# A hybrid decoder layer on one core: products of q's and k's norms three block products behind, a second buffer for u3 in the second set, k's normalisation written beside the last 16 pairs

## The chip, the cores and the metric

The kernel runs on one core of one Trainium2 chip. The metric is the device time of one execution in microseconds (us). Before the change it is 2805.34 us, the median of three runs (2804.27 to 2805.68). One further execution was profiled; it took 2804.28 us. Everything below is float32, computed as products of a rounded high part and a low part (`hi`, `lo`), so that each product of matrices is three matmuls.

## The reference, cut to what matters

```python
h = rms_norm(x, ln_gain)                       # x: 1024 x 2048
proj = h @ w_in                                # 2048 x 10240
q, k, v, z_att, u, z_ssm, g_att, g_ssm = split(proj)   # 1024 wide each, g_*: 2048
q = rms_norm(q.reshape(.., 8, 2, 64), q_norm_gain)
k = rms_norm(k.reshape(.., 8, 2, 64), k_norm_gain)
attn = rms_norm(diff_attention(q, k, v, lam), subln_gain) * (1 - lam_init)
y_att = attn * silu(z_att)
y_ssm = s5_branch(u, ...) * silu(z_ssm)
m = sigmoid(g_att) * (y_att @ w_pa) + sigmoid(g_ssm) * (y_ssm @ w_ps)
x = x + m @ w_out
```

The change touches the first product, `h @ w_in`, in the half of it that finishes the columns, and the root mean squares of q and k that are taken while those columns come out.

## The kernel before

**Tiling.** `h @ w_in` is made in pairs of column blocks: 40 pairs n of 256 columns, and for each pair two halves of the 2048 rows of `w_in`. A pair of one half is a two-by-two block product done in Strassen's manner, with seven block products instead of eight (`pair`, L502). A block product is a call of `products` (L486): 12 matmuls of 128x512 into one PSUM bank. The seven of a pair run in this written order: A11 into bank `pa`, S2 into `pb`, then the last two (A22 and S4) of the pair before, then A12 into `pa`, S1 into `pc`, S3 into `pb`. After A11, S2 and S3 ScalarE copies the bank to SBUF, as `p1`, `u2` and `u3`; the trace names these tiles `p` and `u`. A22 of a pair adds to the same bank `pb` out of which `u3` was just copied, so it can't start before that copy (L523) is done.

**Two sets.** In the first set the pairs are multiplied with one half of the rows and their four outputs go to DRAM (`part`, d_p). In the second set, 36 pairs that are called in the loop at L1044, the same pairs are multiplied with the other half; the first half's output comes back into a tile `q` (L555), is added on GpSimd and VectorE, and each of the four outputs of a pair is handed to a function of its kind (`whole`, L548). In order of the loop's index i: q (4 pairs), k (4), v (4), z_att (4), z_ssm (4), g_att (8), g_ssm (8).

**What is done with the outputs.** For q, `evac_q` (L986) scales and splits the output into `sh_` (ScalarE, L990) and `sl_` (VectorE, L991), stores both, and calls `norms` (L968). For k, `evac_k` stores the output and calls `norms`. `norms` squares the output (`sq`), splits the square into another `sh_` and `sl_` (L90, L91), and adds two matmuls (L975) with a selecting matrix that sum the squares into a bank `nps`. There are two buffers of `sh_` and one of `sl_`. v is transposed and split; z_att and z_ssm go through a sigmoid and a multiplication on GpSimd (L1034, L1035); the gates g through a sigmoid.

**The normalisation of k.** `qk_norms` (L953) makes the inverse root mean squares from `nps`. `norms_k` (L999) is a generator of 16 steps: load a block of k and its factors (`ks`, `rb`; one buffer each), multiply on VectorE (L1015), split into `sh_` and `sl_`, store both, load the next.

**What sets the order.** In this stage each engine's instruction stream is laid out when the program is built, by a scheduler which goes by the dependencies and a timeline of its own; an instruction that stands late in the text is placed early where its inputs are there early. On the chip each engine runs its stream in that order. All DMAs are issued on SyncE's queue, in order too.

Of the kernel before, what the change touches and what calls it, by code (L numbers as in the profile page):

```python
# [10 lines left out]
F32 = mybir.dt.float32  # L11
F32R = mybir.dt.float32r
# [7 lines left out]
P = 128  # L20
# [47 lines left out]
def hybrid_block(ctx: ExitStack, tc: tile.TileContext, x_t, x_n, w_t, w_v, w_glu, w_pa, w_ps,  # L68
                 w_out, small, lams, ssm_bc, out):
    nc = tc.nc  # L70
    V, A, Q, T, D = nc.vector, nc.scalar, nc.gpsimd, nc.tensor, nc.sync
# [17 lines left out]
    def split(hi, lo, src, eng=None):  # L89
        A.activation(hi, src, AF.Copy)  # L90
        (eng or V).tensor_tensor(lo, src, hi.bitcast(F32), ALU.subtract)  # L91
# [11 lines left out]
    def newton_rsqrt(pool, y, v, n):  # L103

        s = pool.tile(list(v.shape), F32, name=n + "_s", tag=n + "_s", bufs=1)
        yi = y.bitcast(I32)
        V.tensor_scalar(yi, v.bitcast(I32), 1, None, ALU.arith_shift_right)
        V.tensor_scalar(yi, yi, -1.0, float(0x5F3759DF), ALU.mult, ALU.add)
        for _ in range(4):
            V.tensor_tensor(s, y, y, ALU.mult)  # L110
            V.tensor_tensor(s, s, v, ALU.mult)
            V.tensor_scalar(s, s, -0.5, 1.5, ALU.mult, ALU.add)
            V.tensor_tensor(y, y, s, ALU.mult)
# [90 lines left out]
    sel = const.tile([P, 160], F32R, name="sel")  # L204
# [55 lines left out]
    def run(steps):  # L260
        for _ in steps:
            pass
# [63 lines left out]
    with ExitStack() as pa_ctx:  # L326
        wp = pa_ctx.enter_context(tc.tile_pool(name="wp", bufs=1, side="right"))
        post = pa_ctx.enter_context(tc.tile_pool(name="post", bufs=1, side="right"))
# [154 lines left out]
        def gain(k):  # L483
            return sm[:, C_LNG + k:C_LNG + k + 1]

        def products(ps, i, a, w, start):  # L486
            hs, ls = a
            wh, wl = w[i]
            for j in range(4):
                c = slice(j * P, (j + 1) * P)  # L490
                for n, (x, y) in enumerate(((wh, hs), (wh, ls), (wl, hs))):
                    T.matmul(ps, lhsT=x[:, c], rhs=y[i][j], start=(start and j == 0 and n == 0),  # L492
                             stop=(j == 3 and n == 2), skip_group_check=True)

        pending = []

        def finish():

            if pending:
                pending.pop()()  # L500

        def pair(w, a, out11, out21, out22, out12):  # L502


            def bank():
                return acc.tile([P, 512], F32, name="acc", tag="acc")
            pa = bank()
            products(pa, A11, a, w, True)
            p1 = post.tile([P, 512], F32, name="p1", tag="p1", bufs=2)
            A.activation(p1, pa, AF.Copy)  # L510
            pb = bank()
            products(pb, S2, a, w, True)
            u2 = post.tile([P, 512], F32, name="u2", tag="u2", bufs=2)
            A.activation(u2, pb, AF.Copy)  # L514
            finish()
            products(pa, A12, a, w, False)
            out11(pa)
            pc = bank()
            products(pc, S1, a, w, True)
            V.tensor_tensor(pc, pc, p1, ALU.subtract)  # L520
            products(pb, S3, a, w, False)
            u3 = post.tile([P, 512], F32, name="u3", tag="u3")
            A.activation(u3, pb, AF.Copy)  # L523
            out22(pc, u3)

            def rest():
                products(pb, A22, a, w, False)
                out21(pb, p1)
                products(pc, S4, a, w, False)
                out12(pc, u2)  # L530
            pending.append(rest)
# [410 lines left out]
        xp_ctx.close()  # L942
        ev_ctx = ExitStack()
        stg = ev_ctx.enter_context(tc.tile_pool(name="stg", bufs=2, side="right"))
        qp = ev_ctx.enter_context(tc.tile_pool(name="qp", bufs=8, side="right"))


        rq = const.tile([P, 16, NT], F32, name="rq")
# [1 line left out]
        nps = [sps.tile([P, 512], F32, name=f"nps{t}", tag=("v", "y")[t]) for t in range(2)]  # L950
        n_norms = [0, 0]

        def qk_norms():  # L953

            for t in range(2):
                v = stg.tile([32, 512], F32, name="nv", tag="sq")
                y = stg.tile([32, 512], F32, name="ny", tag="ny", bufs=1)
                V.tensor_scalar(v, nps[t][0:32], 1.0 / 64, EPS, ALU.mult, ALU.add)
                newton_rsqrt(stg, y, v, "nr")
                D.dma_start(d_rk[:, t * 512:(t + 1) * 512], y[16:32])  # L960
                yield
                tp = sps.tile([P, 4, 32], F32, name="rqp", tag="tr", bufs=2)
                for j in range(4):
                    T.transpose(tp[:, j], y[:, j * P:(j + 1) * P], ident[0:32, 0:32])
                V.tensor_copy(rq[:, :, 4 * t:4 * t + 4].rearrange("p a t -> p t a"), tp[:, :, 0:16])
            V.tensor_scalar(nrq, rq, -1.0, None, ALU.mult)

        def norms(src, row, t):  # L968

            sq = stg.tile([P, 512], F32, name="sq", tag="sq")  # L970
            A.activation(sq, src, AF.Square)
            hi, lo = split_tiles()
            split(hi, lo, sq)
            for n, m in enumerate((hi, lo)):
                T.matmul(nps[t], lhsT=sel[:, 32 - row:160 - row], rhs=m,  # L975
                         start=(n_norms[t] == 0), stop=(n_norms[t] == 31), skip_group_check=True)
                n_norms[t] += 1

        def store2(dst, hi, lo):
            for d_, s_ in zip(dst, (hi, lo)):  # L980
# [2 lines left out]
        def split_tiles():  # L983
            return (stg.tile([P, 512], F32R, name="sh_", tag="sh_"),
                    stg.tile([P, 512], F32R, name="sl_", tag="sl_", bufs=1))
# [9 lines left out]
        def evac_k(h, t, st):  # L995
            D.dma_start(d_k[h, :, t * 512:(t + 1) * 512], st)
            norms(st, 16 + 2 * h, t)
# [46 lines left out]
        for i, (kind, n) in enumerate(order):  # L1044
            f, m = evacs[kind], n - first[kind]
            whole(n, a, 0, lambda c, t, st, f=f, m=m: f(2 * m + c, t, st), qp, None, w)
            w = None
            if n == 8:
                steps = qk_norms()
            if n in (8, 10, 12):  # L1050
                next(steps, None)
            if i == 12:
                ks = norms_k()
            if i >= 12:
                next(ks, None)
        finish()
        ev_ctx.close()
        hp_ctx.close()
        sps_ctx.close()
# [52 lines left out]
        for t in range(2):  # L1112
            tk = slice(t * 512, (t + 1) * 512)
            ya = act_half(act, yg_inputs(t))
            for ct in range(8):
# [3 lines left out]
                for b in range(2):  # L1119
                    raw = wp.tile([P, 4, P], F32, name="w_raw", tag="w_raw", bufs=5)  # L1120
                    D.dma_start(raw, w_glu[ct, :, 4 * b:4 * b + 4])
                    m = (2 * ct + b) % 7
                    hi, lo = (wp.tile([P, 4, P], F32R, name=n, tag=f"{n}{m}") for n in ("w_hi", "w_lo"))
# [15 lines left out]
                hi, lo = (gl.tile([P, 512], F32R, name=n, tag=n, bufs=2) for n in ("yh", "yl"))  # L1139
# [13 lines left out]
    with ExitStack() as at:  # L1153
# [111 lines left out]
        with tc.manual_schedule(engines={T.engine}):  # L1265
            for h in range(H):
# [3 lines left out]
                for n, tt in enumerate(ORDER):  # L1270
                    i = h * NT + n
# [62 lines left out]
    for t in range(2):  # L1334
# [14 lines left out]
        for cb in range(4):  # L1349
            ps = [po.tile([P, 512], F32, name="o", tag="o") for _ in range(4)]  # L1350
            for k in range(KT):
                wh, wl = load_w(w_out[cb, :, k:k + 1], 1, None, wp2)
                for i in range(4):
                    tt = slice(i * P, (i + 1) * P)
                    for n, (a, w) in enumerate(((mh, wh), (mh, wl), (ml, wh))):
                        T.matmul(ps[i], lhsT=a[k][:, tt], rhs=w[:, 0],  # L1356
                                 start=(k == 0 and n == 0), stop=(k == KT - 1 and n == 2))
# [82 lines left out]
```

## Time and profile before

| what | value |
|---|---|
| median of 3 runs | 2805.34 us |
| the profiled execution | 2804.28 us |
| its span, first to last instruction | 2802.5 us |
| TensorE's mean granted clock | 0.985 |
| matmul records in the span | 12402 |
| first and last row of k's multiplication (L1015) | 1253.0 and 1423.9 us |

The span is the time between the first and the last instruction of the profiled execution, 1.8 us less than its own time. In the second set the outputs of q come out in the stretch from some 1000 to 1120 us, those of z_att and z_ssm between some 1290 and 1430 us, and the last 16 pairs after that. Busy time of TensorE in the profile is a union of overlapping matmuls, so a stretch that is 100% busy may still hold matmuls at half the granted clock; the count of matmuls in a stretch tells more than its busy share.

### The profile page before, as it was taken

How to read it: one execution, taken by the hardware profiler on the slowest of the kernel's cores; microseconds unless marked ns; L12 is line 12 of the kernel's file. 1: busy time of each engine (PE TensorE's matmuls, PEld its weight loads, DVE VectorE, ACT ScalarE, POOL GpSimd, SP SyncE). 2: the span in 40 equal slices, each digit the busy share in tenths (PEclk: the TensorE clock that was granted, in tenths of full speed). 3: DMA queues.
4: the chain of work that ended last, by engine and by line, in shares of the span. 5: the costliest groups of instructions: out<-in, count | busy, mean ns of one | idle time of the engine just before them, and what ended most of it. 6: DMA issues, size and time to landing. Idle time of an engine off the chain costs nothing. (4 is left out here: it accounts for less than half of the span.)

```text
span 2802.5 us, 37947 instructions
## 1 busy us (share of the span) xinstructions
PE 2695.5 (96%) x12402; PEld 2205.5 (79%) x12402; DVE 1844.1 (66%) x3512; ACT 1205.9 (43%) x2359; POOL 743.7 (27%) x1101
## 2 busy tenths in 40 slices
PE   9999999999999998998899999789999999999999
PEld 8888788887878876776678888667878778888887
DVE  4998877777787776787676666457666575325432
ACT  6433455545455544433444444345555433223221
POOL 0002866565674011224442222212222200000000
PEclk9999999999999999999999999999999999999999
DMA  9653333333333454457765555976777386455453
GB/s 350 220 180 115 103 113 117 115 116 120 121 101 117 166 181 165 149 174 230 243 214 167 168 162 169 317 234 194 198 238 206 128 296 194 131 155 177 150 158 113
DMA packets 261926, 487.82 MB, mean 174 GB/s; under 512 B 33912, under 2 KB 44480, under 8 KB 261728
## 3 DMA queue, kind: packets, MB, share of 16 engines
q1 hardware_dynamic: 261728, 485.40, 53.7%
q8 instruction: 98, 1.61, 0.2%
q14 instruction: 100, 0.82, 0.1%
HBM read 345.72 MB, written 139.56 MB: 173 GB/s over the span
## 5 line engine op out<-in xcount | busy, mean ns | idle before, releaser
L492 PE MATMUL acc<-ah,w_hi 128*128 128x512 f32 x2128 | 841.6, 396 | 28.1 <-ACT u L523 22.8
L492 PE MATMUL acc<-ah,w_lo 128*128 128x512 f32 x2128 | 841.0, 396 | 0.0
L492 PE MATMUL acc<-al,w_hi 128*128 128x512 f32 x2128 | 840.2, 395 | 0.0
L90 ACT ACTIVATE w_hi<-w_raw 128x512 fp32r<-128x512 f32 x532 | 333.9, 629 | 523.3 <-PE o L1356 219.7
L91 DVE TENSOR_TENSOR w_lo<-w_raw,w_hi 128x512 fp32r<-128x512 f32 x474 | 338.4, 715 | 308.9 <-ACT w_hi L90 296.3
L492 PEld LDWEIGHTS acc<-ah,w_hi 128*128 128x128 f32 x2128 | 402.7, 189 | 120.6 <-ACT u L523 27.6
L492 PEld LDWEIGHTS acc<-ah,w_lo 128*128 128x128 f32 x2128 | 402.5, 189 | 87.7 <-issue 5.4
L492 PEld LDWEIGHTS acc<-al,w_hi 128*128 128x128 f32 x2128 | 402.9, 189 | 83.4 <-issue 2.0
L90 ACT ACTIVATE w_hi<-value 128x512 fp32r<-128x512 f32 x304 | 191.7, 630 | 313.3 <-DVE value L346 161.4
L91 DVE TENSOR_TENSOR w_lo<-value,w_hi 128x512 fp32r<-128x512 f32 x304 | 219.5, 722 | 61.3 <-ACT w_hi L90 53.7
L1356 PE MATMUL o<-w_lo,mh 128*128 128x512 f32 x512 | 199.2, 389 | 0.0
L1356 PE MATMUL o<-w_hi,ml 128*128 128x512 f32 x512 | 199.2, 389 | 0.0
L1356 PE MATMUL o<-w_hi,mh 128*128 128x512 f32 x512 | 195.3, 389 | 0.0
L581 POOL TENSOR_TENSOR u<-u,q 128x512 f32<-128x512 f32 x72 | 99.8, 1387 | 230.2 <-ACT u L514 120.7
L346 DVE TENSOR_TENSOR value<-w_raw 128x512 f32<-128x512 f32 x152 | 150.3, 989 | 2.7
L1185 DVE TENSOR_SCALAR_CACHE_REDUCE pe<-s,nrq 128x128 f32<-128x128 f32 (+7 forms) x128 | 100.1, 813 | 70.9 <-PE s L1181 58.9
L91 POOL TENSOR_TENSOR w_lo<-w_raw,w_hi 128x512 fp32r<-128x512 f32 x58 | 84.0, 1448 | 234.3 <-ACT w_hi L90 204.0
L575 POOL TENSOR_TENSOR p<-p,q 128x512 f32<-128x512 f32 x36 | 60.5, 1680 | 322.5 <-DVE acc L520 210.0
L288 PE MATMUL pc<-ah,w_hi 128*128 128x512 f32 x256 | 107.6, 420 | 25.4 <-DVE z L292 16.8
L1187 ACT ACTIVATE pe<-pe,mx 128x128 f32<-128x128 f32 (+7 forms) x128 | 98.5, 773 | 42.2 <-DVE pe L1185 42.0
L1356 PEld LDWEIGHTS o<-w_lo,mh 128*128 128x128 f32 x512 | 96.1, 188 | 20.0
L1356 PEld LDWEIGHTS o<-w_hi,mh 128*128 128x128 f32 x512 | 96.1, 188 | 19.9
(681 smaller groups left out, 4588.5 us busy)
## 6 DMA issues: line engine op xcount, KB each, us to landing
w_raw<-in_w_t_dram SPq DMA_DIRECT2D x288, 256.0 KB
q<-d_p SPq DMA_DIRECT2D x160, 256.0 KB
w_raw<-in_w_out_dram SPq DMA_DIRECT2D x128, 256.0 KB
d_p<-u SPq DMA_DIRECT2D x72, 256.0 KB
w_raw<-in_w_ps_dram SPq DMA_DIRECT2D x64, 256.0 KB
w_raw<-in_w_pa_dram SPq DMA_DIRECT2D x64, 256.0 KB
d_p<-ps SPq DMA_DIRECT2D x52, 256.0 KB
d_p<-p SPq DMA_DIRECT2D x36, 256.0 KB
```

Source lines behind the costliest of these rows:

```text
L90: A.activation(hi, src, AF.Copy)
L91: (eng or V).tensor_tensor(lo, src, hi.bitcast(F32), ALU.subtract)
L288: T.matmul(ps, lhsT=w[:, k % 4], rhs=b[k], start=(k == 0 and n == 0), stop=(k == 7 and n == 2))
L346: V.tensor_tensor(t, x, y, ALU.add)
L492: T.matmul(ps, lhsT=x[:, c], rhs=y[i][j], start=(start and j == 0 and n == 0), stop=(j == 3 and n == 2), skip_group_check=True)
L575: e.tensor_tensor(u, u, other(1), ALU.add)
L581: e.tensor_tensor(u, u, other(i), ALU.subtract)
L1185: V.tensor_scalar(pc[c][:, 0:w], sc[c][:, 0:w], nrq[:, 2 * h + c, tt:tt + 1], None, ALU.mult, ALU.min, accum_out=mx[:, c:c + 1])
L1187: ins = A.activation(pc[c][:, 0:w], pc[c][:, 0:w], AF.Exp, bias=mx[:, c:c + 1], scale=-1.0, accum_out=su[:, c:c + 1])
L1356: T.matmul(ps[i], lhsT=a[k][:, tt], rhs=w[:, 0], start=(k == 0 and n == 0), stop=(k == KT - 1 and n == 2))
```

## The change

There are four edits.

1. `norms` no longer places its two matmuls at once. It appends them to a list, and `products` emits what is due: a matmul pair is emitted at the start of the third block product after the one that is current. The square's parts get tiles of their own, `nh` and `nl`, two buffers each, so that `sh_` and `sl_` are left to `evac_q`, `evac_v` and `norms_k`.
2. In the second set `u3` is taken in turns from the old place and from a second one, so there are two buffers.
3. To make room, the tiles `q` get 5 buffers in place of 8, and `ny` shares a buffer with `rb`.
4. `qk_norms` starts one pair later (its inputs come later), and `norms_k` is started at i = 20 in place of i = 12; its last step is run after the loop.

```diff
+        tick, postponed = [0], []
+
         def products(ps, i, a, w, start):
+            tick[0] += 1
+            while postponed and postponed[0][0] <= tick[0]:
+                postponed.pop(0)[1]()
...
-        pending = []
+        pending, turn, more = [], [0], []
...
-            u3 = post.tile([P, 512], F32, name="u3", tag="u3")
+            turn[0] ^= 1
+            if more and turn[0]:
+                u3 = more[0].tile([P, 512], F32, name="u3", tag="u3", bufs=1)
+            else:
+                u3 = post.tile([P, 512], F32, name="u3", tag="u3")
...
-        qp = ev_ctx.enter_context(tc.tile_pool(name="qp", bufs=8, side="right"))
+        more.append(stg)
+        qp = ev_ctx.enter_context(tc.tile_pool(name="qp", bufs=5, side="right"))
...
-                y = stg.tile([32, 512], F32, name="ny", tag="ny", bufs=1)
+                y = stg.tile([32, 512], F32, name="ny", tag="rb", bufs=1)
...
-            hi, lo = split_tiles()
+            hi, lo = (stg.tile([P, 512], F32R, name=n, tag=n) for n in ("nh", "nl"))
             split(hi, lo, sq)
-            for n, m in enumerate((hi, lo)):
-                T.matmul(nps[t], lhsT=sel[:, 32 - row:160 - row], rhs=m,
-                         start=(n_norms[t] == 0), stop=(n_norms[t] == 31), skip_group_check=True)
-                n_norms[t] += 1
+
+            def add():
+                for m in (hi, lo):
+                    T.matmul(nps[t], lhsT=sel[:, 32 - row:160 - row], rhs=m,
+                             start=(n_norms[t] == 0), stop=(n_norms[t] == 31), skip_group_check=True)
+                    n_norms[t] += 1
+            postponed.append((tick[0] + 3, add))
...
-            if n == 8:
+            if n == 9:
                 steps = qk_norms()
-            if n in (8, 10, 12):
+            if n in (9, 11, 13):
                 next(steps, None)
-            if i == 12:
+            if i == 20:
                 ks = norms_k()
-            if i >= 12:
+            if i >= 20:
                 next(ks, None)
         finish()
+        run(ks)
```

The changed program's lines are numbered higher: L497 is the matmul of `products`, L987 that of the norms, L1004 evac_q's low part, L1028 k's multiplication.

**First place: TensorE, in the q pairs.** Before, in the third q pair: the end of S3 into bank acc_11394, four matmuls of the norms, and A22 into the same bank.

```order
L492 MATMUL acc_11394<-al_10952,w_hi_11366 128x512
L492 MATMUL acc_11394<-ah_10951,w_lo_11367 128x512
L975 MATMUL nps0_11009<-sl__11252,sel_65 128x512
L975 MATMUL nps0_11009<-sh__11278,sel_65 128x512
L975 MATMUL nps0_11009<-sl__11279,sel_65 128x512
L975 MATMUL nps1_11010<-sh__11322,sel_65 128x512
L492 MATMUL acc_11394<-ah_10960,w_hi_11371 128x512
L492 MATMUL acc_11394<-al_10961,w_hi_11371 128x512
```

After, one pair further on: the end of S3 into acc_11600, with the start of A11 of the next pair into acc_11791.

```order
L987 MATMUL nps0_11009<-nh_11665,sel_65 128x512
L497 MATMUL acc_11600<-al_10952,w_hi_11570 128x512
L497 MATMUL acc_11600<-ah_10951,w_lo_11571 128x512
L497 MATMUL acc_11791<-ah_10845,w_hi_11756 128x512
L497 MATMUL acc_11791<-al_10846,w_hi_11756 128x512
L497 MATMUL acc_11791<-ah_10845,w_lo_11757 128x512
L497 MATMUL acc_11791<-ah_10849,w_hi_11756 128x512
L497 MATMUL acc_11791<-al_10850,w_hi_11756 128x512
L987 MATMUL nps0_11009<-nl_11666,sel_65 128x512
L497 MATMUL acc_11791<-ah_10849,w_lo_11757 128x512
```

Before, S3 and A22 of a pair stand back to back with only the norms' matmuls between them. After, A11 and S2 of the next pair, 24 matmuls, stand between S3 and A22, and the norms' matmuls are strewn among the products: those of S4's output, `nh_11665` and `nl_11666`, have 36 and 44 matmuls between them and the end of that S4.

**Second place: VectorE, in the q pairs.** Before, the low parts of q (L991) and of its square (L91) take the one `sl_` buffer in turn.

```order
L991 SCALAR_TENSOR_TENSOR sl__11452<-u2_11199,gqk_66,sh__11451 128x512
L91 TENSOR_TENSOR w_lo_11959<-w_raw_11952,w_hi_11958 128x512
L91 TENSOR_TENSOR sl__11460<-sq_11457,sh__11459 128x512
L991 SCALAR_TENSOR_TENSOR sl__11479<-q_11328,gqk_66,sh__11478 128x512
L91 TENSOR_TENSOR w_lo_11783<-value_11780,w_hi_11782 128x512
L346 TENSOR_TENSOR value_11962<-w_raw_11950,w_raw_11952 128x512
L91 TENSOR_TENSOR sl__11487<-sq_11484,sh__11486 128x512
```

After, `sl_` is q's alone, and the square's low part is `nl`.

```order
L1004 SCALAR_TENSOR_TENSOR sl__11658<-u2_11405,gqk_66,sh__11657 128x512
L580 TENSOR_TENSOR q_11532<-acc_11583,q_11532 128x512
L91 TENSOR_TENSOR w_lo_11769<-w_raw_11754,w_hi_11768 128x512
L91 TENSOR_TENSOR nl_11666<-sq_11663,nh_11665 128x512
L1004 SCALAR_TENSOR_TENSOR sl__11683<-q_11532,gqk_66,sh__11682 128x512
L525 TENSOR_TENSOR acc_11694<-acc_11694,p1_11598 128x512
L91 TENSOR_TENSOR w_lo_11773<-value_11760,w_hi_11772 128x512
```

The number of instructions is the same; between two uses of the `sl_` buffer there are now three other instructions, and none of them takes the buffer.

**Third place: VectorE, where k is multiplied.** Before, in the third pair of z_att (i = 14):

```order
L1015 TENSOR_TENSOR ks_14247<-ks_14247,rb_14249 128x512
L366 TENSOR_TENSOR value_13914<-value_13914,w_raw_13906 128x512
L571 TENSOR_TENSOR q_13712<-acc_13763,q_13712 128x512
L91 TENSOR_TENSOR w_lo_13921<-w_raw_13906,w_hi_13920 128x512
L91 TENSOR_TENSOR sl__14422<-ks_14247,sh__14421 128x512
L520 TENSOR_TENSOR acc_13846<-acc_13846,p1_13776 128x512
L91 TENSOR_TENSOR w_lo_13925<-value_13912,w_hi_13924 128x512
L346 TENSOR_TENSOR value_13928<-w_raw_13900,w_raw_13904 128x512
L91 TENSOR_TENSOR w_lo_13931<-value_13928,w_hi_13930 128x512
L1015 TENSOR_TENSOR ks_14427<-ks_14427,rb_14429 128x512
```

After, in the fourth pair of z_att (i = 15):

```order
L1028 TENSOR_TENSOR ks_15555<-ks_15555,rb_15557 128x512
L366 TENSOR_TENSOR value_14053<-value_14053,w_raw_14045 128x512
L580 TENSOR_TENSOR q_13863<-acc_13914,q_13863 128x512
L91 TENSOR_TENSOR w_lo_14060<-w_raw_14045,w_hi_14059 128x512
L91 TENSOR_TENSOR sl__15722<-ks_15555,sh__15721 128x512
L525 TENSOR_TENSOR acc_13997<-acc_13997,p1_13927 128x512
L91 TENSOR_TENSOR w_lo_14064<-value_14051,w_hi_14063 128x512
L346 TENSOR_TENSOR value_14067<-w_raw_14039,w_raw_14043 128x512
L91 TENSOR_TENSOR w_lo_14070<-value_14067,w_hi_14069 128x512
L1028 TENSOR_TENSOR ks_15727<-ks_15727,rb_15729 128x512
```

Nothing moved within the piece; it stands one pair later. Counted by the rows of pc - p1 (L520, L525), of which every pair has one, 76 in all and 36 in the second set, the 16 multiplications of k stand before behind the 52nd to the 59th such row, and after behind the 54th to the 60th. Those are the pairs i = 12 to 19 before (from the second step on i = 13) and i = 14 to 20 after, z_att and z_ssm but for the last, though the changed text starts `norms_k` at i = 20. The order of ScalarE and SyncE there is likewise the same but for the shift, and behind the second set all streams stand as before, but for an exchange of neighbours here and there. Between its first and its last multiplication of k VectorE's stream has now 123 rows for 16 steps; before, it had 118 from the second step to the sixteenth.

## The prediction

> **What bounds the kernel now.** I read the page first, then the busy time by stretches, then what TensorE (PE) waits for in the stretches that lose time, and last the timelines behind those waits. The page gives the frame:
>
> ```profile
> PE 2695.5 (96%) x12402; PEld 2205.5 (79%) x12402; DVE 1844.1 (66%) x3512; ACT 1205.9 (43%) x2359; POOL 743.7 (27%) x1101
> ```
>
> TensorE is the bound; only the time in which it stands or runs slowly can be won. Four stretches of the second set, with each engine's busy time and count, the granted clock and the share of DMA:
>
> ```profile
> 975.00:1130.00 155.00, 137.53 (x558) 108.94 (x557) 109.84 (x152) 74.28 (x129) 26.11 (x18) 0.93 0.50 168
> 1130.00:1200.00 70.00, 70.00 (x313) 57.59 (x312) 49.63 (x69) 34.22 (x60) 14.75 (x10) 1.00 0.42 140
> 1290.00:1430.00 140.00, 119.32 (x484) 93.46 (x483) 97.68 (x126) 54.42 (x97) 58.11 (x42) 0.95 0.74 240
> 1430.00:1700.00 270.00, 270.00 (x1192) 223.54 (x1192) 180.65 (x231) 120.19 (x201) 68.27 (x48) 1.00 0.53 169
> ```
>
> The last is undisturbed: 270 us / 1192 matmuls = 0.2265 us for one, and 84 x 0.2265 = 19.03 us for a pair. At that pace the 558 matmuls of the first stretch (q) would take 126.4 us of 155, so 28.6 us are lost there; the 484 of the third (z_att and z_ssm) 109.6 of 140, so 30.4. Together 59.0 us, 2.1% of the span, are the most that the edits can touch. What PE waits for, in the first stretch and then in z_att and z_ssm:
>
> ```profile
> PE acc L492 <- ACT u L523: 5.9, 5, 1.5
> PE nps L975 <- DVE sl__11279 L91: 3.5, 1, 3.5
> PE nps L975 <- DVE sl__11695 L91: 3.5, 1, 3.5
> PE nps L975 <- DVE sl__11487 L91: 3.4, 1, 3.4
> ```
> ```profile
> PE acc L492 <- ACT u L523: 15.8, 6, 4.3
> PE acc L492 <- DVE q L571: 3.1, 4, 1.6
> ```
>
> The waits in the first make some 16 us, not 28.6. PE's timeline shows the rest:
>
> ```profile
> 1035.74 0.40 PE L975 MATMUL nps<-sh__11278,sel 128*128 128x512 f32 x1
> 1039.68 0.50 PE L975 MATMUL nps<-sl__11279,sel 128*128 128x512 f32 x1 [3.54 <-DVE sl__11279 L91]
> 1042.33 0.80 PE L492 MATMUL acc<-ah,w_hi 128*128 128x512 f32 x1 [1.41 <-ACT u L523]
> 1043.34 0.63 PE L492 MATMUL acc<-ah,w_lo 128*128 128x512 f32 x1
> 1043.77 0.63 PE L492 MATMUL acc<-ah,w_hi 128*128 128x512 f32 x1
> 1048.31 0.40 PE L492 MATMUL acc<-ah,w_hi 128*128 128x512 f32 x1
> ```
>
> After the wait a matmul starts every 0.43 us (1043.34 to 1043.77) instead of 0.23, until 1048.31: a long wait is followed by some 5 us at half the clock, which costs 2 to 3 us more.
>
> **Term 1: q's norms (edits 1 and 2).** Why was `sl__11487`, the low part of a square, late?
>
> ```profile
> 1065.60 0.75 DVE L991 SCALAR_TENSOR_TENSOR sl__11479<-q,gqk,sh__11478 128x512 fp32r<-128x512 f32 x1 [2.25 <-PE nps L975]
> 1068.49 0.69 DVE L91 TENSOR_TENSOR sl__11487<-sq,sh__11486 128x512 fp32r<-128x512 f32 x1 [0.81 <-DMA d_q<-sl__11479]
> ```
> ```profile
> 1066.37 0.32 SPq L981 DMA_DIRECT2D d_q<-sl__11479  x1
> ```
>
> The one buffer goes from VectorE to a store, back to VectorE, to PE and back: VectorE waits for PE's norm matmul, then for the store (issued at 1066.37, done when the next row starts, 2.1 us later), and PE waits for VectorE. The order puts exactly these matmuls between S3 and A22, where PE has nothing else. The change takes both away. The squares get `nh` and `nl`, held only until PE has read them. The norms' matmuls have 36 and 44 others between them and the product whose square they sum: 36 x 0.2265 = 8.2 us. The chain they wait for is an output's VectorE operation, the square, its copy and its low part, four operations of 0.6 to 0.75 us, so some 3 us; 5 us remain for what queues ahead on ACT and DVE. And S3 and A22 of a pair have 24 matmuls between them, 5.4 us, for the copy of u3 to come. No arithmetic is added: the same 64 norm matmuls stay on PE's path. The most won is 28.6 us. The least: DVE works 109.8 of 155 us there and keeps `sl_` in one buffer for q, so each of the four q pairs could still lose a wait as long as those of 3.5 us with some 2.5 us of half clock, 4 x 6 = 24 us; only 4 to 5 us would be won. I take 4 us left (a wait of 1 us in each q pair, without the half clock), nearer to the upper end, because the k pairs, whose squares take the same path without a store of `sl_`, lose nothing (313 matmuls in the 70 us of the second row above): **-24.6 us**.
>
> **Term 2: k's normalisation (edit 4).** The stretch of z_att and z_ssm loses its time otherwise. One of its stalls, on DVE, ACT and PE:
>
> ```profile
> 1319.59 0.69 DVE L1015 TENSOR_TENSOR ks<-ks,rb 128x512 f32<-128x512 f32 x1 [3.26 <-DMA ks<-d_k]
> 1324.42 1.64 DVE L346 TENSOR_TENSOR value<-w_raw 128x512 f32<-128x512 f32 x1
> ```
> ```profile
> 1326.15 0.63 ACT L90 ACTIVATE w_hi<-value 128x512 fp32r<-128x512 f32 x1 [3.42 <-DVE value L346]
> 1326.69 0.58 ACT L523 ACTIVATE u<-acc 128x512 f32<-128x512 f32 x1
> ```
> ```profile
> 1327.32 0.50 PE L492 MATMUL acc<-ah,w_hi 128*128 128x512 f32 x1 [2.72 <-ACT u L523]
> ```
>
> PE names u3's copy, but ACT was held in its order by a weight's copy, that by a sum on DVE, and DVE by `ks`, whose load was late. k's multiplications run as a loop: load, multiply, split, store, next load, with one buffer of `ks`.
>
> ```profile
> 1290.37 0.69 DVE L1015 TENSOR_TENSOR ks<-ks,rb 128x512 f32<-128x512 f32 x1 [2.23 <-DMA rb<-d_rk]
> 1423.88 0.69 DVE L1015 TENSOR_TENSOR ks<-ks,rb 128x512 f32<-128x512 f32 x1 [1.15 <-DMA d_zs<-q]
> ```
> ```profile
> DVE ks L1015 <- DMA ks<-d_k: 23.0, 10, 6.1
> ```
>
> The second step is at 1290.37, the sixteenth at 1423.88: 14 intervals of 9.54 us, a little over two to a pair of 19.03, and PE must keep that pace because DVE runs in order. This ends at the moment in which the stalls end. The text now starts the loop at i = 20, but the streams don't: its 16 steps stand beside i = 14 to 20, in the same pattern, one pair later. So the mechanism stays. It even holds one step more in as long a piece: 15 intervals (143 us) over 123 DVE rows, where 14 took 118 rows. Of the 9.54 us more, the three further rows that aren't k's carry 3 / 16 of a pair (16 DVE rows besides k's), 3.6 us. Bounds: 9.5 us lost if the loop binds at every step, and all 30.4 won if it binds nowhere; I take **+4 us**, by the nearest rows, those of the same loop.
>
> [...]
>
> **Term 3: u3's second buffer in z_att and z_ssm.** Its effect in the q pairs is in term 1. Here u3 is copied at 1326.69 (above) and its last reader before the store is
>
> ```profile
> 1332.35 1.30 POOL L1035 TENSOR_TENSOR u<-u,sg 128x512 f32<-128x512 f32 x1 [3.66 <-ACT sg L1034]
> ```
> ```profile
> 1334.23 0.41 SPq L1038 DMA_DIRECT2D d_za<-u  x1
> ```
>
> With some 2 us for the store as above, it is free 10 us after the copy, and needed again after a pair, 19. **0 us**; at the very most the 15.8 us of waits that name u3.
>
> **Term 4: five buffers of q for eight, `ny` in `rb`'s place, the last step behind the loop.** Loads of q are then issued one pair ahead instead of two. A load of 256 KB lands in at most some 6 us (the wait above) of 19, so the pair before covers it. The last step of the loop stands beside i = 20 anyway. **0 us**; if the cover went, see the slower rival.
>
> **Sum.** -24.6 + 4 = -20.6 us. On the profiled execution, 2804.28 - 20.6 = 2783.7 us (span 2781.9). The median shown is 1.06 us above that execution, so on its scale 2784.7; I say **2785 us**.
>
> **The rivals.**
>
> *u3 was the limit in z_att and z_ssm.* The waits name it (15.8 us), and the second buffer would end them and their half clock: 30.4 us more, and without the 4 us of term 2: 2785 - 34.4 = 2751 us. Its life of 10 us speaks against it. The Trainium skill (Trainium Kernel Development and Optimization, Best Practices) recommends double buffers to overlap transfers with work, which would put the gain here. Chance 4%.
>
> *The k loop binds less.* One pair later it meets other loads, and the pattern may slip by half a step; if a third of the 30.4 us goes instead of 4 us being added: 2785 - 14 = 2771 us. Chance 13%.
>
> *The norms' wait comes back in another form.* The norms' matmuls are strewn through PE's order; if ACT and DVE run more than 5 us behind, PE waits at each, and half of term 1 is lost: 2785 + 12 = 2797 us. For it: DVE is busy 71% there, with `sl_` still waiting for its store; against it: the k pairs. Chance 18%.
>
> *Slower: q's loads hold up SyncE's queue.* A load of q that waits for its buffer holds the weights behind it. With the pair's buffers freed later than the weights are needed, each of 36 pairs would lose that; from 20.6 / 36 = 0.57 us a pair on, the change is slower than before, and with the 2.1 us of a store in each, 36 x 2.1 = 76 us, it takes 2861 us. Against it: in the undisturbed stretch PE never waits for a weight. Chance 4%, and as much again for something between, about no change.
>
> **How the numbers follow.** The forecast, 2785 us, has 57%, the rest as above. What a measurement of this kernel can tell from no change is some 0.2%, 5.6 us. The range 2768 to 2798 takes in term 1's and term 2's likely errors and the rivals at 2771 and 2797; it leaves out 2751 and the slower case, with some of the tails. Faster by over 0.2% means below 2799.7: all but the slower cases, 0.91; within 0.2%: 0.05; slower: 0.04.
>
> **What would show it.** Right: in the q pairs no wait of PE for `sl_`, `nh` or `nl` above 1 us, no half clock, and 558 matmuls in some 130 us; k's 16 multiplications (L1028) some 9.5 us apart beside z_att and z_ssm, with PE's waits there still named after u3's copy; the last 15 pairs at 19.03 us. Wrong: waits of PE at L987, or k's loop spread over the last 16 pairs, or PE waiting for weights.

## The result, and the profile after

| kernel | median of its runs | ratio to before, 95% interval |
|---|---|---|
| before | 2804.81 us (2803.65 to 2805.68) | |
| changed | 2777.99 us (2775.64 to 2783.51) | 0.9907 [0.989, 0.9925] |

Both medians are of four executions; before, these are the three of the first table and one more. The change takes off about 26 us. The profiled execution of the changed kernel is the slowest of its four, 2783.51 us (span 2781.7). In the experiments below one execution, of e9, was slow (3017.05 us) and is left out.

TensorE's line of the page, after, has the same number of matmuls and less busy time:

```profile
PE 2689.2 (97%) x12402; PEld 2203.8 (79%) x12402; DVE 1848.7 (66%) x3512; ACT 1205.7 (43%) x2359; POOL 738.9 (27%) x1101
```

Busy time by stretches, after, in the columns used before (PE, PEld, DVE, ACT and POOL with their counts, the granted clock, the DMA share, GB/s). The stretches are q's pairs, the 140 us of z_att and z_ssm in which k's loop runs (11 us earlier than before), and the last pairs of the set:

```profile
975.00:1130.00 155.00, 152.31 (x659) 122.49 (x658) 127.84 (x179) 87.88 (x154) 32.58 (x22) 1.00 0.58 188
1279.00:1419.00 140.00, 117.09 (x483) 91.30 (x482) 96.56 (x123) 54.10 (x96) 57.59 (x41) 0.98 0.74 240
1420.00:1690.00 270.00, 269.77 (x1191) 223.25 (x1190) 178.54 (x231) 120.83 (x203) 66.00 (x46) 1.00 0.53 171
```

In the first row 659 matmuls stand where 558 stood; at 0.2265 us each they need 149.3 us, so 5.7 us are lost where 28.6 were, and the clock is 1.00 where it was 0.93. In the second, 140 - 483 x 0.2265 = 30.6 us are lost, against 30.4 before, at the same DMA share. The third loses nothing, as before. The change has emptied one stretch and left the other as it was.

What PE waits for after, in q's pairs, and then in z_att and z_ssm (total, times, longest, us):

```profile
PE nps L987 <- DVE nl L91: 2.6, 4, 1.3
```
```profile
PE acc L497 <- ACT u L532: 16.6, 6, 4.3
PE acc L497 <- DVE u L591: 2.7, 3, 1.7
```

The waits of 3.4 to 3.5 us for `sl_` and the half clock behind them are gone. The waits that name u3's copy in z_att and z_ssm are still there, though u3 has two buffers now. Behind them stands k's loop, in the rows of its multiplications and in what VectorE waits for, its two largest rows:

```profile
L1028 DVE TENSOR_TENSOR ks<-ks,rb x16: 678/693/1576, 1278.7 to 1419.2; 128x512 f32<-128x512 f32 x16
```
```profile
DVE ks L1028 <- DMA ks<-d_k: 19.5, 9, 4.6
DVE ks L1028 <- DMA q<-d_p: 16.1, 4, 6.5
```

Sixteen multiplications in 140.5 us make 15 intervals of 9.37 us. The text says "beside the last 16 pairs"; the second row of the stretches has 483 matmuls between the first and the last step, 483 / 84 = 5.75 pairs. VectorE waits before 15 of the 16 multiplications, 39.5 us in all: the 13 waits shown, one of 2.8 us for `rb` and one of 1.1 us that names a store. The multiplication doesn't read `q`, so which transfer ended the four waits that name a load of `q` is not certain.

### The profile page after: what moved, and what is told of

Read it like the earlier page. It is cut to its first block, busy times and chain, and to the rows that moved or that the text cites. A ratio compares the mean times of both kernels' runs of the same rounds, so it can differ in the third digit from the quotient of the medians.

```text
span 2781.7 us, 37927 instructions
## 1 busy us (share of the span) xinstructions
PE 2689.2 (97%) x12402; PEld 2203.8 (79%) x12402; DVE 1848.7 (66%) x3512; ACT 1205.7 (43%) x2359; POOL 738.9 (27%) x1101
## 4 chain that ended last, share of the span: by engine, by line
PE 79%; DMA 8%; DVE 7%; issue 2%; POOL 2%; ACT 1%; SPq 1%; DVEq 0%; ACTq 0%; POOLq 0%
PE acc L497 41%; PE o L1370 12%; PE pc L271 6%; PE pc L288 5%; PE acc L476 3%; PE s L1192 2%; PE op L1229 2%; DMA ks<-d_k 1%; PE pg L1149 1%; DVE w_lo L91 1%; PE tp L1217 1%; DMA w_raw<-in_w_ps_dram 1%; DMA kl<-d_k 1%; DMA q<-d_p 1%; PE gp L853 1%
## 5 line engine op out<-in xcount | busy, mean ns | idle before, releaser
L497 PE MATMUL acc<-ah,w_hi 128*128 128x512 f32 x2128 | 838.5, 394 | 25.1 <-ACT u L532 18.5
L497 PE MATMUL acc<-ah,w_lo 128*128 128x512 f32 x2128 | 838.6, 395 | 0.0
L497 PE MATMUL acc<-al,w_hi 128*128 128x512 f32 x2128 | 837.6, 394 | 0.0
L91 DVE TENSOR_TENSOR w_lo<-w_raw,w_hi 128x512 fp32r<-128x512 f32 x474 | 334.4, 707 | 298.8 <-ACT w_hi L90 280.3
L497 PEld LDWEIGHTS acc<-ah,w_hi 128*128 128x128 f32 x2128 | 400.9, 188 | 117.8 <-ACT u L532 22.8
L497 PEld LDWEIGHTS acc<-ah,w_lo 128*128 128x128 f32 x2128 | 400.7, 188 | 86.5 <-issue 5.4
L497 PEld LDWEIGHTS acc<-al,w_hi 128*128 128x128 f32 x2128 | 400.9, 188 | 82.6 <-issue 2.0
L91 DVE TENSOR_TENSOR w_lo<-value,w_hi 128x512 fp32r<-128x512 f32 x304 | 222.7, 733 | 61.5 <-ACT w_hi L90 53.8
L91 POOL TENSOR_TENSOR w_lo<-w_raw,w_hi 128x512 fp32r<-128x512 f32 x58 | 84.0, 1449 | 236.2 <-ACT w_hi L90 204.7
L1370 PEld LDWEIGHTS o<-w_hi,ml 128*128 128x128 f32 x512 | 96.2, 188 | 19.8
```

The lines of the kernel that those rows point to most:

```text
L1370: T.matmul(ps[i], lhsT=a[k][:, tt], rhs=w[:, 0], start=(k == 0 and n == 0), stop=(k == KT - 1 and n == 2))
```

## The experiments

All are compared with the kernel before (medians of 2802.4 to 2803.2 us in these comparisons). Losses in a stretch are its length less its matmuls at 0.2265 us, from the profiled execution of each kernel. q's pairs are read from 975 to 1130 us; the gates' stretch is that of z_att and z_ssm, from 1260 to 1430 us. In the latter before has 625 matmuls and loses 28.4 us, and the changed kernel has 610 and loses 31.8:

```profile
1260.00:1430.00 170.00, 149.32 (x625) 117.84 (x624) 123.59 (x168) 65.74 (x118) 70.83 (x48) 0.96 0.74 241
```
```profile
1260.00:1430.00 170.00, 146.15 (x610) 114.48 (x609) 122.57 (x156) 66.43 (x119) 73.09 (x51) 0.98 0.71 230
```

### Which edit emptied q's pairs

**e1_defer_only**: the changed kernel with one u3 in the second set.

```diff
-            turn[0] ^= 1
-            if more and turn[0]:
-                u3 = more[0].tile([P, 512], F32, name="u3", tag="u3", bufs=1)
-            else:
-                u3 = post.tile([P, 512], F32, name="u3", tag="u3")
+            u3 = post.tile([P, 512], F32, name="u3", tag="u3")
```

> The changed kernel without u3's second buffer: every output of the second set uses the one u3 again; the norms stay three block products behind, with nh and nl. Theory N (the gain lies in the norms' products and their own buffers): the first stretch, q's pairs, keeps its 5 us of loss in place of 28.6, and the time is that of the changed kernel, 2778 us, within 4 (2774 to 2782). Rival U (u3's second buffer carries part of the gain): the waits of PE that name u3's copy in q's pairs, 5.9 us before, come back with their half clock, and the time is 2786 to 2797 us. In z_att and z_ssm both expect no difference from the changed kernel if u3 isn't the limit there; if it is, the loss of some 30 us there grows.

Measured: 2779.0 us, ratio 0.9912 [0.9898, 0.9925]. q's pairs, by stretch:

```profile
975.00:1130.00 155.00, 153.14 (x667) 124.25 (x666) 129.63 (x181) 88.65 (x155) 33.16 (x22) 1.00 0.58 188
```

3.9 us are lost. The changed kernel keeps its whole gain without the second u3.

**e2_u3_only**: the kernel before with the second u3 and five `q` buffers.

```diff
+            turn[0] ^= 1
+            if more and turn[0]:
+                u3 = more[0].tile([P, 512], F32, name="u3", tag="u3", bufs=1)
+            else:
+                u3 = post.tile([P, 512], F32, name="u3", tag="u3")
-            u3 = post.tile([P, 512], F32, name="u3", tag="u3")
...
-        qp = ev_ctx.enter_context(tc.tile_pool(name="qp", bufs=8, side="right"))
+        more.append(stg)
+        qp = ev_ctx.enter_context(tc.tile_pool(name="qp", bufs=5, side="right"))
```

> The kernel before with u3's second buffer in the second set and five buffers of q for eight; norms as before, k's loop as before. Theory N: the time of before, 2804 us, within 4, with the waits for sl_ of 3.4 to 3.5 us still in q's pairs. Rival U: 2780 to 2795 us, with the losses in z_att and z_ssm or in q's pairs smaller by 10 us or more.

Measured: 2791.41 us, ratio 0.9956 [0.9942, 0.9969]: 12 us, which theory N didn't expect. The stretch, and what PE waits for in it:

```profile
975.00:1130.00 155.00, 146.03 (x607) 114.73 (x606) 118.48 (x165) 78.74 (x137) 29.91 (x20) 0.98 0.54 177
```
```profile
PE acc L492 <- ACT p L510: 5.4, 3, 1.9
PE acc L492 <- ACT u L527: 1.8, 4, 0.5
PE nps L980 <- DVE sl__11115 L91: 0.6, 1, 0.6
```

17.5 us are lost in place of 28.6. The long waits for `sl_` went though its buffer is as before: in e2's stream the matmul with `sl__11487` stands 25 instructions behind the one with `sh__11486`, where before it stood right behind it. So the scheduler's order moved with the edit. Of the waits shown, those for `sl_` shrank from 10.4 to 0.6 us and those for u3 from 5.9 to 1.8, while waits of 5.4 us for another copy (`p`) came in; whether the order or the free buffer brought the gain was not parted. The second u3 is a weaker remedy for the same loss; together with the other it adds nothing (e1).

**e9_q5_only** splits e2: only `bufs=8` to `bufs=5`.

```diff
-        qp = ev_ctx.enter_context(tc.tile_pool(name="qp", bufs=8, side="right"))
+        qp = ev_ctx.enter_context(tc.tile_pool(name="qp", bufs=5, side="right"))
```

> The kernel before with five buffers of q in place of eight and nothing else. It splits the kernel with u3's second buffer, 2791 us, into its two edits. Theory U (of those 12 us u3's second buffer has all): 2803 us, within 4. Rival Q (the five buffers move the order of the loads and of the norms, and that gives it): 2791 us, within 4.

Measured: 2802.77 us over eleven executions, ratio 1.0009 [0.9996, 1.0021]. No cost or gain of the five buffers can be measured; e2's 12 us need the second u3.

**e5_own_only** and **e6_defer_split** part edit 1, both with one u3: e5 has the squares' own tiles without the deferral, e6 the deferral without the tiles.

```diff
-            def add():
-                for m in (hi, lo):
-                    T.matmul(nps[t], lhsT=sel[:, 32 - row:160 - row], rhs=m,
-                             start=(n_norms[t] == 0), stop=(n_norms[t] == 31), skip_group_check=True)
-                    n_norms[t] += 1
-            postponed.append((tick[0] + 3, add))
+            for m in (hi, lo):
+                T.matmul(nps[t], lhsT=sel[:, 32 - row:160 - row], rhs=m,
+                         start=(n_norms[t] == 0), stop=(n_norms[t] == 31), skip_group_check=True)
+                n_norms[t] += 1
```
```diff
-            hi, lo = (stg.tile([P, 512], F32R, name=n, tag=n) for n in ("nh", "nl"))
+            hi, lo = split_tiles()
```

> The changed kernel without the deferral and without u3's second buffer: the squares have nh and nl of their own, but the norms' matmuls are issued right behind the square, as before. Theory B (the one low-part buffer, which VectorE, its store, the square and TensorE take in turn, is what made the wait): PE's waits for the norms in q's pairs stay under 1 us on average, the stretch loses 10 us or less, and the time is 2779 to 2786 us. Rival P (the place of the norms' matmuls, right behind a square that is not yet there, makes it): they wait 2 to 3.5 us in each q pair with the half clock behind, and the time is 2793 to 2803 us.

> The changed kernel without own buffers for the squares and without u3's second buffer: the norms' matmuls are three block products behind, but the squares share sh_ and sl_ with the outputs. Theory B: sl_ is now held until those matmuls have run, 8 us and more, and VectorE waits for it twice in each output: q's pairs lose as much as before or more, 28 us and up, and the time is 2800 us or more. Rival P: the deferral alone brings the gain, 2779 to 2786 us.

Measured: e5 2777.2 us, 0.991 [0.9896, 0.9923]; e6 2811.17 us, 1.0024 [1.0014, 1.0034]. The same stretch in e5 and then in e6:

```profile
975.00:1130.00 155.00, 153.59 (x667) 124.21 (x666) 130.33 (x180) 89.79 (x157) 33.42 (x22) 1.00 0.59 190
```
```profile
975.00:1130.00 155.00, 138.13 (x553) 108.25 (x552) 108.16 (x151) 73.38 (x128) 25.90 (x18) 0.92 0.48 161
```

e5 loses 3.9 us, e6 29.7. What VectorE waits for in e6, two rows of many:

```profile
DVE sl__11475 L1000 <- PE nps L983: 2.5, 1, 2.5
DVE sl__11529 L91 <- DMA d_q<-sl__11521: 2.2, 1, 2.2
```

and PE in turn:

```profile
PE nps L983 <- DVE sl__11483 L91: 3.4, 1, 3.4
```

The circle of the kernel before is all there: VectorE waits for PE's norm matmul, then for the store out of the same buffer, and PE for VectorE. The buffers of the squares are the whole gain; the deferral of the title, without them, brings none, and e6 is 0.1 to 0.3% slower than before. Both kernels hold edits 3 and 4, so these don't make the gain by themselves either.

### What makes the loss in z_att and z_ssm

**e3_paced**: the load of `ks` waits for the latest u3 copy, so that the loop goes one step a pair from i = 20, as the text says.

```diff
-            A.activation(u3, pb, AF.Copy)
+            copies.append(A.activation(u3, pb, AF.Copy))
...
-                D.dma_start(st, d_k[h, :, t * 512:(t + 1) * 512])
+                after(D.dma_start(st, d_k[h, :, t * 512:(t + 1) * 512]), copies[-1])
```

> The changed kernel with one thing more: each load of ks waits for u3's copy of the pair before it, so that k's loop really goes one step a pair over the last 16 pairs, where it stood 2 to 3 steps a pair beside pairs 14 to 20. Theory K (k's loop, through VectorE's order, makes the loss in z_att and z_ssm): the 30 us lost there fall to under 8, none appears in the last 16 pairs, and the time is 2778 - 25 = 2753 us (2748 to 2760). Rival U (u3, or the gates' own work, makes it): the loss stays, and the time is 2778 us, within 4. Rival S (a load that waits holds the weights behind it in SyncE's queue): PE waits for weights' sums in the last 16 pairs, over 0.6 us a pair, and the time is above 2763 us.

**e4_paced16**: the same from i = 16.

```diff
-            if i == 20:
+            if i == 16:
                 ks = norms_k()
-            if i >= 20:
+            if i >= 16:
                 next(ks, None)
```

> As the paced kernel, but the loop begins beside pair 16, so that half of its steps stand beside z_att and z_ssm, one a pair, and the last is done four pairs before the end. Theory K (what stalls is more than one step in a pair, not a step beside the gates): 2753 us, as the paced one from pair 20, within 4. Rival G (any step of k's loop beside the gates' work costs, since the gates' loads and stores make ks late): its steps beside z_att and z_ssm cost some 30 / 16 = 1.9 us each, and the time is about 2760 us or more.

Measured: e3 2756.88 us, 0.9833 [0.9818, 0.9848]; e4 2745.93 us, 0.98 [0.9786, 0.9813]. The gates' stretch in e3 and then in e4:

```profile
1260.00:1430.00 170.00, 169.41 (x749) 139.65 (x749) 127.98 (x155) 75.69 (x129) 81.62 (x57) 1.00 0.53 178
```
```profile
1260.00:1430.00 170.00, 169.41 (x749) 139.63 (x748) 138.68 (x159) 73.57 (x130) 79.10 (x57) 1.00 0.59 197
```

170 - 749 x 0.2265 = 0.4 us are lost in both, where the changed kernel loses 31.8. Theory K holds, and rival G falls at this density: in e4, with a step every 19.4 us from 1328.3 on, six stand in this stretch, and it is as clean as in e3, whose loop begins at 1405 us and has two there. VectorE waits in e4 no less than before:

```profile
L1028 DVE TENSOR_TENSOR ks<-ks,rb x16: 691/693/1358, 1328.3 to 1618.6; 128x512 f32<-128x512 f32 x16
```
```profile
DVE ks L1028 <- DMA ks<-d_k: 30.4, 11, 5.5
DVE ks L1028 <- issue: 19.8, 5, 4.8
```

VectorE stands 50.2 us before the 16 steps, 3.1 us on average; 11 of these waits are put down to the load of `ks`, and for 5 ("issue") the profile shows nothing that was waited for. But there is one in each 19.4 us, and over all the steps PE loses 300 - 1323 x 0.2265 = 0.3 us:

```profile
1320.00:1620.00 300.00, 299.81 (x1323) 247.92 (x1323) 228.81 (x279) 130.10 (x233) 90.61 (x63) 1.00 0.66 218
```

So VectorE has that much slack once in a pair; with two or three steps in a pair, as in the changed kernel, it has not.

e3 and e4 should have been equal within 4 us and are 11 apart. The difference lies behind the set's last product, in the 100 us that follow it, e3 and then e4:

```profile
1699.00:1799.00 100.00, 79.84 (x306) 61.55 (x305) 40.91 (x58) 36.86 (x62) 19.55 (x15) 0.88 0.89 273
```
```profile
1696.00:1796.00 100.00, 85.57 (x351) 66.84 (x350) 51.79 (x63) 38.54 (x66) 26.67 (x18) 0.93 0.90 296
```

45 matmuls fewer, 45 x 0.2265 = 10.2 us. ScalarE, which makes the next stage's weights, waits for their loads from 1690 to 1790 us, e3 and then e4:

```profile
ACT w_hi L90 <- DMA w_raw<-in_w_glu_dram: 29.8, 10, 9.6
```
```profile
ACT w_hi L90 <- DMA w_raw<-in_w_glu_dram: 15.6, 6, 6.7
```

In e3 the loop's last multiplication starts at 1696.7 us, two before the set's last product. SyncE's queue issues the twelfth of these loads at 1720.75 us in e3 and at 1703.02 us in e4:

```profile
1720.75 1.46 SPq L1135 DMA_DIRECT2D w_raw<-in_w_glu_dram  x1
```
```profile
1703.02 0.42 SPq L1135 DMA_DIRECT2D w_raw<-in_w_glu_dram  x1
```

Ahead of it e3's queue stands 4.1 us for the loop's last store:

```profile
SPq L1141 <- DMA d_k<-sl__17486: 4.1, 1, 4.1
```

The rest is order: between the eleventh and the twelfth stand 24 other DMAs in e3's stream and 4 in e4's. So the late end of the loop delays the next stage's weights in the queue (rival S, but in the next stage), in part by a wait and in part by another order; no run tested it apart from the start of the loop.

**e7_paced16_one_u3**: e4 with one u3 (the edit of e1).

> The paced kernel from pair 16, without u3's second buffer. Theory (u3's buffer is worth nothing once the norms are deferred and k's loop is paced): 2746 us, within 4. Rival U (with k's stalls gone, u3 is the next limit beside the gates): the waits of PE that name u3's copy in z_att and z_ssm, the 16 pairs without a loss in the paced kernel, come back, and the time is 2752 us or more.

Measured: 2746.02 us, 0.9792 [0.9779, 0.9805]: e4's time. All that PE waits for in the gates' stretch:

```profile
PE acc L497 <- ACT u L528: 0.6, 1, 0.6
```

With k's loop paced, one buffer of u3 is enough beside the gates.

**e8_before_paced16**: the kernel before with the pace and the start at i = 16 alone (the edits of e3 and e4, and `run(ks)` behind the loop).

> The kernel before with nothing but k's loop begun beside pair 16 and paced by u3's copies, one step a pair; norms, u3 and the buffers of q as before. Theory K (two independent losses of some 30 us in separate stretches): 2804 - 33 = 2771 us, within 5, with q's stretch still losing 28 us and z_att and z_ssm under 5. Rival D (the gains depend on each other: with one u3 and the norms as before the gates' pairs stall all the same): 2785 us or more.

Measured: 2771.43 us, 0.9883 [0.9868, 0.9898]. q's pairs and the gates' stretch:

```profile
975.00:1130.00 155.00, 137.74 (x555) 108.74 (x555) 109.72 (x153) 74.03 (x128) 26.20 (x18) 0.92 0.49 165
1260.00:1430.00 170.00, 170.00 (x759) 140.52 (x760) 145.47 (x170) 72.06 (x127) 83.44 (x57) 1.00 0.59 199
```

q still loses 29.3 us, the gates nothing. The two losses are independent: 1.17% here and 0.88% in e1 make 2.05%, and e7, which has both, has 2.08%.

**e10_ks_rb_two**: the changed kernel with one u3, no pace, and two buffers of `ks` and of `rb` (and of `ny`, which shares rb's place).

```diff
-                st = stg.tile([P, 512], F32, name="ks", tag="ks", bufs=1)
+                st = stg.tile([P, 512], F32, name="ks", tag="ks", bufs=2)
...
-                rb = stg.tile([P, 512], F32, name="rb", tag="rb", bufs=1)
+                rb = stg.tile([P, 512], F32, name="rb", tag="rb", bufs=2)
```

> The changed kernel with two buffers of ks and of rb, no pace, and without u3's second buffer: the loads are issued a step ahead, and the order has the 16 steps in 5 pairs, some 6 us a step. Theory K1 (the loop's own length of 9.5 us, load, multiply, split, load again, against an order that has nearly three steps in a pair of 19 us): with the load a step ahead the loop keeps up, the loss in z_att and z_ssm falls from 31 to under 10 us, and the time is 2750 to 2760 us. Rival K2 (three steps a pair are too much for the DMA queues or VectorE beside the gates, whatever the lead): VectorE still waits for ks or rb, the loss stays above 20 us, and the time is 2768 us or more.

Measured: 2765.03 us, 0.9868 [0.9847, 0.9889], between the two. Its loop:

```profile
1239.00:1348.00 109.00, 96.90 (x410) 77.24 (x409) 91.86 (x111) 45.32 (x81) 45.73 (x31) 0.97 0.84 280
```
```profile
L1024 DVE TENSOR_TENSOR ks<-ks,rb x16: 678/692/1822, 1239.7 to 1347.9; 128x512 f32<-128x512 f32 x16
```
```profile
DVE ks L1024 <- DMA rb<-d_rk: 6.5, 4, 3.4
```

A step takes 108.2 / 15 = 7.2 us instead of 9.4, and 109 - 410 x 0.2265 = 16.1 us are lost instead of 30.6; the wait for `ks` has nearly gone. About half of the loss is the load's lead; the other half remains while the steps stay as dense. What holds it was not tested: VectorE now waits for `rb` and, up to 3.4 us at a time, for the stores out of the one buffer of `sl_`, and the DMA share is 0.84. Each theory holds for a half. The Trainium skill (Trainium Kernel Development and Optimization, Best Practices) recommends double buffers to overlap transfers with work. The measurement agrees: they win 14 us here (e10 against e1). Spacing the steps with single buffers wins 33 (e7 against e1).

**e11_own_paced12**: e5's edit with the pace from i = 12, one u3.

```diff
-            if i == 20:
+            if i == 12:
                 ks = norms_k()
-            if i >= 20:
+            if i >= 12:
                 next(ks, None)
```

> The smallest change that should have it all: own buffers nh and nl for the squares, no deferral, one u3, and k's loop paced by u3's copies from pair 12 on, so that all its steps but the last few stand beside z_att and z_ssm. Theory K: 2746 us, within 4. Rival G (steps beside the gates cost after all when all of them stand there, or the first two, which share a pair, do): 2752 us or more.

Measured: 2759.73 us, 0.9847 [0.9829, 0.9864]: rival G, 14 us slower than e7. Around its first two steps (1274.1 and 1282.7 us) and behind them, in e11 and then in e7, whose loop has not begun in the first row:

```profile
1280.00:1304.00 24.00, 19.80 (x79) 15.29 (x78) 18.73 (x21) 9.13 (x17) 9.87 (x7) 0.93 0.69 234
1304.00:1430.00 126.00, 124.55 (x546) 101.62 (x545) 108.82 (x118) 54.20 (x98) 56.03 (x40) 1.00 0.63 213
```
```profile
1280.00:1304.00 24.00, 24.00 (x108) 19.87 (x107) 19.95 (x23) 9.38 (x17) 14.41 (x10) 1.00 0.53 183
1304.00:1430.00 126.00, 126.00 (x558) 104.33 (x557) 101.94 (x115) 55.93 (x98) 54.55 (x39) 1.00 0.62 207
```

The place where two steps share a pair loses 29 matmuls, 6.6 us; the stretch behind it 12 more, 2.7 us, though e7 has steps there too. e11 also lacks the deferral, which was worth nothing in e5 and acts on q's and k's pairs only. In the profiled executions the set's last product starts 9.4 us later than in e7 (1704.98 against 1695.59 us) and the span is 10.9 us longer (2757.3 against 2746.4). The rest of the 14 us is the distance of these executions from their medians: e7's was 2.2 us above, e11's 0.7 below.

**e12_k_late_only**: the kernel before with k's start written at i = 20 alone.

```diff
-            if i == 12:
+            if i == 20:
                 ks = norms_k()
-            if i >= 12:
+            if i >= 20:
                 next(ks, None)
         finish()
+        run(ks)
```

> The kernel before with the text's start of k's loop at i = 20 in place of 12 and nothing else. Theory (the order has the loop where it was, so the edit does nothing): 2804 us, within 4, with some 30 us lost in z_att and z_ssm. Rival (it does what it says): z_att and z_ssm lose under 10 us and the time is 2785 us or less.

Measured: 2801.11 us, 0.9991 [0.998, 1.0002], and the gates' stretch:

```profile
1260.00:1430.00 170.00, 151.64 (x630) 120.15 (x630) 124.06 (x169) 67.58 (x120) 74.43 (x49) 0.95 0.72 243
```

27.3 us are lost, where before loses 28.4 in the same stretch. The loop stands where it stood before (1253.0 to 1423.9 us):

```profile
L1015 DVE TENSOR_TENSOR ks<-ks,rb x16: 691/694/1293, 1250.9 to 1421.8; 128x512 f32<-128x512 f32 x16
```

The edit does not do what its text says, and is worth nothing that can be measured.

## Why the prediction was right, and where it was not

2785 us was forecast and 2777.99 measured, within the range. The sum was made on the profiled execution: 2783.7 us against 2783.51. That it came within 0.2 us is luck. The second set's last product starts at 1752.86 us before and at 1728.43 after, so 24.4 us were won up to there, 3.8 more than the sum's 20.6; and in this execution the later stage took 3.6 us longer than before. Of the signs one was missed: PE waits up to 1.3 us for `nl` at L987, where a wait above 1 us was to count against the prediction.

**Term 1 was right in size, and half of its reasons were not needed.** 5.7 us are left in this profile, 3.9 in e1 and e5; 4 were forecast. The reason that held is the first one: one buffer of `sl_` shared by VectorE, its store, the square and PE (e6 keeps it and loses 29.7 us, e5 removes it and loses 3.9). The prediction gave the deferral a part, with 8.2 us of cover; e5 has none and is as fast. It also put u3's second buffer into this term without a number; without the squares' buffers it is worth 12 us (e2), beside them nothing (e1).

**Term 2 had the mechanism and mis-sized the sum by 4 us**: "+4" was measured as +0.2 in the 140 us compared (30.6 against 30.4). The step that failed is the price of the one close interval more. The prediction's own count of VectorE rows gives 9.54 - 3.6 = 5.9 us for it; it took 4 "by the nearest rows" and doesn't say how 5.9 becomes 4. From step to step, before from the second to the sixteenth and after from the first to the sixteenth:

```profile
1290.37:1423.88 133.51, 113.10 (x458) 88.59 (x457) 91.82 (x118) 50.72 (x90) 54.91 (x39) 0.95 0.74 238
```
```profile
1278.70:1419.20 140.50, 117.59 (x485) 91.69 (x484) 96.81 (x123) 54.10 (x96) 57.79 (x41) 0.98 0.73 240
```

Before, 14 intervals of 9.54 us hold 7.4 us of PE's work each and lose 133.51 - 458 x 0.2265 = 29.8 us. After, 15 intervals of 9.37 us hold 7.3 and lose 140.5 - 485 x 0.2265 = 30.7. That is some 2.1 us an interval both times; the further one came with its own work for PE, so it cost about 1 us by this count. This is the loss written another way and no test of it. The test is in e3 and e4: where a step gets 19 us of PE's time, the loss is gone.

**Term 3**, 0 us, is shown by e7 against e4 (2746.02 and 2745.93) and e1 against the changed kernel. The rival that u3 was the limit beside the gates falls: two buffers left the waits that name it, and the pace removed them with one.

**Term 4**, 0 us, is shown for the five buffers by e9 and for the start of k's loop by e12. `ny` in `rb`'s place and the later start of `qk_norms` were not run alone.

**What the forecast on the median missed** is 7 us. The set gained 3.8 us more than the sum says, which is about what term 2 had too much. The rest is how far one execution lies from the next: the changed kernel's four take from 2775.64 to 2783.51 us, and the profiled one was 5.5 us above their median. The later stage, whose code no edit touches, in the profile of the changed kernel and then of e1, which took 2778.72 us:

```profile
1750.00:2300.00 550.00, 491.53 (x2448) 409.70 (x2447) 349.66 (x749) 255.65 (x546) 122.25 (x87) 0.95 0.73 222
```
```profile
1750.00:2300.00 550.00, 492.38 (x2469) 409.28 (x2468) 352.92 (x755) 257.18 (x549) 121.70 (x87) 0.96 0.74 224
```

21 matmuls, 4.8 us, lie between two executions that entered it within 0.5 us of each other. What varies there was not found.

**The best version** is the paced one from i = 16 with one u3 (e7), 2746.02 us, 2.08% below before. It needs the squares' own tiles and the pace; whether the deferral can go from it too was not run.

## What to carry to other kernels

When a tile's one buffer is passed round between a store and three engines, give the later user a tile of its own before moving instructions about: here the tile was the whole gain and the move none. A loop of load, work and store that hangs in an engine's order should be judged by the time that the order leaves for a step against the time that a step takes; if the second is longer, tie the load to an event of the main work, since where the text starts the loop may not move it. Such a loop is better ended some pairs before the next stage's loads begin; e4 against e3 suggests this, and no run tested it alone.

## What was not expected of the hardware

VectorE can stand some 3 us for a late load once in a pair of 19 us without any loss on TensorE (e4: 50.2 us of waits in 16 steps, 0.3 us lost), while two or three such waits in a pair go with 31 us lost in all (39.5 us of waits in the changed kernel). The later stage differed by 4.8 us between two executions (the changed kernel and e1) whose streams there are the same but for a few exchanged neighbours; 5.6 us was the whole bound for no change.
